# The loop for overfull experts moves from behind step 20 to behind step 4 of the expert stage, and constants move ahead of the first activation

## The chip, the cores and the metric

The kernel runs on one core of one Trainium2 chip. The metric is the device time of one execution in microseconds (us). Three runs of the kernel before took 1916.12, 1918.36 and 1924.67 us; the median is 1918.36 us. In the texts PE is TensorE, DVE is VectorE, ACT is ScalarE, POOL is GpSimd and SP is SyncE; a q behind the name is the engine's sequencer.

## The reference, cut to what matters

Two blocks run one after the other on 256 tokens of 1024 values, all in float32. The first is an attention block with a mixture of experts; the second has two layers, each with a mixer and an MLP. The change lies in the mixture of experts:

```python
logits = t @ w_router + b_router                 # 256 tokens, 32 experts
top_val, top_idx = lax.top_k(logits, 4)          # each token goes to 4 experts
gate_w = softmax(top_val)
# for every expert e and the tokens that chose it:
hb = xb @ w_exp_in[e] + b_exp_in[e]              # 1024 -> 2048
g, u = minimum(hb[:, :1024], 7.0), clip(hb[:, 1024:], -7.0, 7.0)
a = g * sigmoid(1.702 * g) * (u + 1.0)
y = a @ w_exp_out[e] + b_exp_out[e]              # 1024 -> 1024
# every token: the sum of its 4 results by gate_w, then h = layer_norm(alpha * h + sum)
```

The mean load of an expert is 32 tokens, but the router decides, so an expert can have more.

## The kernel before, in words

**The expert stage.** It is written as `step(0)` to `step(32)`. Each step handles one expert with room for 64 tokens (`CAP`); step e also finishes expert e-1. The weights of an expert are six tiles of 2 MiB: four of `w_exp_in` and two of `w_exp_out`. In program order a step uses them as in 0, in 1, out 0 and out 1 of the expert before, in 2, in 3. PE first writes the biases (L771), then multiplies the tokens by the in tiles (`up_tile`, L922, into the banks `pg` and `pu`), turns the activation of the expert before (`aT`, L944), multiplies it by the out tiles (`down_tile`, L953, into `py`), and spreads the result back over all tokens (`combine`, L966, into `pc`), where DVE adds it to the running sum `facc` (L971, written over `bcs`). In every odd step PE also gathers the tokens of the next two experts (`gather`, L895, into `xg`); it needs a selection `sel` that DVE computes (L886). At the end of a step DVE and ACT form the activation (`swiglu`, L932 to L938) and DVE the table `sd` for the way back (L904).

**What sets the order.** PE's instructions of the steps are pinned to program order (`keep`). On DVE, ACT and POOL a scheduler places each instruction, and a tile from a pool can be written only when the readers of the buffer's last user are done. The six weight tiles of a step come through one DMA queue, issued by SP in the order in which `get(key)` asks for them. They rotate through eight buffers of 2 MiB (pools `ring`, `ring2`, `ring3`), so SP can issue a load only when PE has used up the tile that lay in that buffer.

**The loop.** An expert with more than 64 tokens needs further passes. `later_consts` works out from the counts a table `tab` with one entry for each further pass, and their number, which lands in `ti[0:1, 16:17]`. After step 20 the kernel issues the seven loads that follow (all six tiles of step 21, and in 0 of step 22), reads the number into a register of every engine (`values_load`, L1154) and enters a loop with that many trips (`tc.For_i`, L1155). Each trip loads an expert's six tiles through `ring3` and does a whole expert. The loop has an entry and an exit at which the engines meet and the counters of the semaphores start anew. In step 20 the activation and `sd` are kept in another pool (`aside`, pool `accp`), as the loop uses `tmp`.

**What else stands in the stage.** `facc_init` (the start of the running sum; it also takes one step of the side work `ada0`) and `later_consts` (the table, masks and triangles for later stages) are emitted after step 0. `load_bo`, `ln2_rows` and `out_bias` follow steps 2, 4 and 6: the load of `b_exp_out` by POOL, four short rows loaded by POOL and spread over 128 partitions by PE (L1003), and the bias product (L1015).

```python
for e in range(21):                                    # L1144
    step(e)
    if e == 0:
        facc_init()
        later_consts()
    elif e in (2, 4, 6):
        {2: load_bo, 4: ln2_rows, 6: out_bias}[e]()
for key in step_tiles(21) + step_tiles(22)[0:1]:       # L1151
    get(key)
with tc.issue_after(mark["SP"]):
    n_over = nc.values_load(ti[0:1, 16:17], min_val=0, max_val=15)
with tc.For_i(0, n_over, 1) as it:                     # L1155
```

Of the kernel before, what the change touches and what calls it, by code (L numbers as in the profile page):

```python
# [18 lines left out]
NE = 32  # L19
# [53 lines left out]
def tile_kernel(  # L73
# [20 lines left out]
    def bank(name="bank", tag="b"):  # L94
        return pp.tile([128, 512], F32, tag=tag, name=name)
# [31 lines left out]
    def wload(src, shape_str, pool=None, parts=1, pin=False, **kw):  # L127
        s = (pool or ring).tile([128, 4096], F32, tag="w", name="w")
        n = 1
        for d in src.shape[1:]:  # L130
            n *= d
        view = s[:, 0:n].rearrange(shape_str, **kw)
        k = src.shape[1] // parts
        for i in range(parts):
            ins = nc.sync.dma_start(view[:, i * k:(i + 1) * k], src[:, i * k:(i + 1) * k])
            mark["SP"] = ins.ins
            if pin:
                keep(ins)
        return view

    def wcols(w, c0, ncol, k0=0, kc=8, pool=None, parts=1, pin=False):
        return wload(w[k0 * 128:(k0 + kc) * 128, c0:c0 + ncol].rearrange("(k p) n -> p k n", p=128),
                     "p (k n) -> p k n", k=kc, pool=pool, parts=parts, pin=pin)
# [621 lines left out]
    def bias_sel(oh):  # L765
        return oh

    def expert_bias(p, oh, half, pin=lambda i: i, halves=(0, 1)):
        for hv in halves:
            q = 2 * half + hv  # L770
            pin(T.matmul(p[64 * hv:64 * hv + 64, :], oh[:, q:q + 1].to_broadcast([128, 64]), bi,  # L771
                         start=True, stop=False))
# [93 lines left out]
    def step_tiles(e):  # L866

        out = [("in", e, 0), ("in", e, 1)] if e < NE else []
        out += [("out", e - 1, i) for i in range(2)] if e else []
        return out + ([("in", e, 2), ("in", e, 3)] if e < NE else [])  # L870
# [3 lines left out]
    def get(key):  # L874
        if key not in loaded:
            kind, e, i = key
            loaded[key] = spare() if key == ("in", 1, 2) else (tin if kind == "in" else tout)(e, i)
        return loaded[key]

    def gather(rank_aps, pin=lambda i: i):  # L880
        n = len(rank_aps)
        xg = wsp.tile([128, 8, 128], F32, tag="wh", name="xg")
        sel = tmp("sel", 256).rearrange("p (t s) -> p t s", t=2)
        for t in range(2):
            for a in range(n):
                mark["sel"] = V.tensor_scalar(sel[:, t, a * 64:(a + 1) * 64], slot_i, rank_aps[a][:, t:t + 1], None,  # L886
                                              op0=ALU.is_equal).ins
        w = 64 * n

        def half(hf):  # L890
            p = bank("xg")
            for kc in range(4):
                i, r = divmod(4 * hf + kc, 2)
                for t in range(2):
                    pin(T.matmul(p[:, kc * 128:kc * 128 + w], h1[:, t, 256 * i + r:256 * (i + 1):2], sel[:, t, 0:w],  # L895
                                 start=t == 0, stop=t == 1))
            S.copy(xg[:, 4 * hf:4 * hf + 4, 0:w], p.rearrange("p (k s) -> p k s", k=4)[:, :, 0:w])  # L897

        return xg, half
# [17 lines left out]
    def up_tile(acc, xg, a, i, w, pin=lambda i: i):  # L917
        pg_, pu_ = acc
        for r, p, b0 in ((0, pg_, 0), (0, pu_, 1024), (1, pg_, 0), (1, pu_, 1024)) if i < 3 else (
                (0, pg_, 0), (1, pg_, 0), (0, pu_, 1024), (1, pu_, 1024)):  # L920
            for hv in range(2):
                last = pin(T.matmul(p[64 * hv:64 * hv + 64, :], xg[:, 2 * i + r, a * 64:(a + 1) * 64],  # L922
                                    w[:, r, b0 + hv * 512:b0 + (hv + 1) * 512], start=False, stop=i == 3 and r == 1))
        mark["up"] = last.ins
# [16 lines left out]
    def down_turn(uc, pin=lambda i: i):  # L941
        p = bank("aT")
        for r in range(4):
            last = pin(T.transpose(p[:, r * 128:(r + 1) * 128], uc[:, r:512:4], ident))  # L944
        mark["aT"] = last.ins
        aT = tmp("aTs")
        S.copy(aT, p)
        return aT

    def down_tile(py, aT, i, w, pin=lambda i: i):  # L950
        for r in range(4):
            for j in range(2):
                pin(T.matmul(py[64 * j:64 * j + 64, :], aT[:, r * 128 + i * 64:r * 128 + (i + 1) * 64],  # L953
                             w[:, r, j * 512:(j + 1) * 512], start=i == 0 and r == 0, stop=i == 1 and r == 3))

    def evict(py):
        ys = tmp("ys")
        S.copy(ys, py)  # L958
        return ys

    def combine(sT, ys, sums=None, pin=lambda i: i):
        for t in range(2):
            pc = []
            for j in range(2):
                p = sums[t, j] if sums else bank("pc")
                pin(T.matmul(p, sT[64 * j:64 * j + 64, t * 128:(t + 1) * 128], ys[64 * j:64 * j + 64, :],  # L966
                             start=not sums, stop=True))
                pc.append(p)
            for j in range(0 if sums else 2):
                f = facc[:, t, j * 512:(j + 1) * 512]  # L970
                V.tensor_tensor(f, f, pc[j], op=ALU.add)  # L971
# [19 lines left out]
    def facc_init():  # L991
        next(ada0, None)
        with tc.issue_after(first_sel):
            for t in range(2):
                V.tensor_scalar(facc[:, t], h1[:, t], ALPHA, None, op0=ALU.mult)
# [93 lines left out]
    def take_sum(t):  # L1089
        for j in range(2):  # L1090
            p = bank("pc", "bg"[t])
            keep(T.matmul(p, ident, facc[:, t, j * 512:(j + 1) * 512], start=True, stop=False))
            sums[t, j] = p

    def step(e):

        w = {key: get(key) for key in step_tiles(e)}
        d = downs.pop(e - 1, None)
        nxt = None
        if e < NE:  # L1100
            acc = first_acc[e] if e < 2 else (bank("pg", "g"), bank("pu", "g"))
            if e > 1:
                eb = bias_sel(ident[:, 4 * e:4 * e + 4])
                expert_bias(acc[0], eb, 0, keep)
                expert_bias(acc[1], eb, 1, keep)
            xg, a = xgs.pop(e)
            up_tile(acc, xg, a, 0, w["in", e, 0], keep)
            if e == 0:
                with tc.issue_after(mark["up"]):
                    xg_, nxt = gather([rr[:, :, 1]], keep)  # L1110
                xgs[1] = xg_, 0
            elif e % 2 and e + 1 < NE:
                with tc.issue_after(mark["up"]):
                    xg_, nxt = gather([rr[:, :, e + 1 + b] for b in range(2)], keep)
                xgs[e + 1], xgs[e + 2] = (xg_, 0), (xg_, 1)
        if nxt:
            nxt(0)
        if d:
            uc, turn = d
            aT = down_turn(uc, keep)  # L1120
        if e < NE:
            up_tile(acc, xg, a, 1, w["in", e, 1], keep)
        else:
            take_sum(1)
        if d:
            sT = turn()
            py = bank("py")
            for i in range(2):
                down_tile(py, aT, i, w["out", e - 1, i], keep)
            ys = evict(py)  # L1130
        if e < NE:
            up_tile(acc, xg, a, 2, w["in", e, 2], keep)
        if nxt:
            nxt(1)
        if d:
            combine(sT, ys, sums if e == NE else None, keep)
        if e < NE:
            up_tile(acc, xg, a, 3, w["in", e, 3], keep)
            if e == NE - 1:
                take_sum(0)  # L1140
            held = aside if e == 20 else tmp
            downs[e] = swiglu(acc, held), spread_sel(rr[:, :, e], gw[:, :, e], keep, held)

    for e in range(21):  # L1144
        step(e)
        if e == 0:
            facc_init()
            later_consts()
        elif e in (2, 4, 6):
            {2: load_bo, 4: ln2_rows, 6: out_bias}[e]()  # L1150
    for key in step_tiles(21) + step_tiles(22)[0:1]:  # L1151
        get(key)
    with tc.issue_after(mark["SP"]):
        n_over = nc.values_load(ti[0:1, 16:17], min_val=0, max_val=15)  # L1154
    with tc.For_i(0, n_over, 1) as it:  # L1155
# [27 lines left out]
        for i in range(2):  # L1183
            down_tile(py, aT, i, tout(eo, i, ring3, False))
        combine(turn(), evict(py))
    for e in range(21, NE + 1):
        step(e)
    w_ahead = [wcols(w_in_ab_2[0], 2048, 512), wcols(w_in_ab_2[0], 1536, 512), wcols(w_in_ab_2[0], 2560, 512)]
    st2.close()

# [497 lines left out]
```

## Time and profile before

| | |
|---|---|
| three runs | 1916.12, 1918.36, 1924.67 us |
| the profiled execution | 1921.77 us, span 1920.0 us |
| PE busy | 1833.3 us, 95% of the span |
| DVE, ACT, POOL busy | 42%, 29%, 5% |
| data moved by DMA | 595.84 MB, of that 540.68 MB on SP's queue |
| the expert stage | about 253 to 1206 us of the span |

The profile is of one execution; its times count from the start of its span. A group of a timeline gives the start of the first of some like instructions, how long the group took, and in brackets how long the engine had stood idle and what released it. L971 appears once in each step from step 1 on, so the distance from one such row to the next is the length of a step.

### The profile page before, as it was taken

What the parts mean: (1) busy time and instruction counts of PE and PEld (TensorE: products, weight loads), DVE (VectorE), ACT (ScalarE), POOL (GpSimd) and SP (SyncE); (2) the same over time, 40 slices, a digit from 0 to 9 for tenths busy, and PEclk for the clock granted to TensorE, in tenths of its full rate; (3) what the DMA queues carried; (4) which work ended last, traced back from release to release, by engine and by line L of the source; (5) the groups of instructions that cost most, each with busy time, mean ns of one, the idle gap of its engine ahead of it and who ended that gap; (6) DMA issues with size and microseconds to landing.
All of it is one profiled execution on the core that took longest, in us unless ns stands there. A gap on an engine that the chain in (4) does not pass through costs nothing.

```text
span 1920.0 us, 23489 instructions
## 1 busy us (share of the span) xinstructions
PE 1833.3 (95%) x9861; PEld 1106.0 (58%) x9861; DVE 799.4 (42%) x1388; ACT 557.3 (29%) x869; POOL 91.1 (5%) x106
## 2 busy tenths in 40 slices
PE   7999989999999999985999999899999999999999
PEld 6867743333333333322333333688888965778997
DVE  6756741121211221220221122667754465665555
ACT  4645301110011110000101110554544454564443
POOL 3000100000000000000000000200100011000000
PEclk9989979998999999997999999999999999999999
DMA  8667868998999999998999999774666565434452
GB/s 291 243 219 264 346 252 330 428 420 360 425 427 428 427 428 427 428 427 336 427 428 427 428 427 416 268 254 148 250 252 249 213 239 179 153 131 154 176 196 89
DMA packets 100302, 595.84 MB, mean 310 GB/s; under 512 B 7533, under 2 KB 8002, under 8 KB 75362
## 3 DMA queue, kind: packets, MB, share of 16 engines
q1 hardware_dynamic: 85874, 540.68, 69.9%
q0 software_dynamic: 14288, 53.63, 8.0%
q8 instruction: 78, 1.28, 0.3%
q14 instruction: 30, 0.25, 0.0%
q10 hardware_dynamic: 32, 0.01, 0.0%
HBM read 593.24 MB, written 1.06 MB: 310 GB/s over the span
## 4 chain that ended last, share of the span: by engine, by line
PE 80%; DMA 8%; issue 5%; DVE 4%; POOL 1%; ACT 1%; SPq 0%; POOLq 0%; DVEq 0%; ACTq 0%
PE pg L922 11%; PE py L953 11%; PE pu L922 11%; PE xg L895 4%; DMA w<-in_w_exp_in_dram 4%; DMA wa<-in_ada_w_dram 3%; PE hid L271 3%; PE hid L270 3%; PE hid L269 3%; PE pc L966 3%; PE acc L254 3%; PE acc L255 3%; PE acc L256 3%; PE adp L628 2%; PE pu L771 2%
## 5 line engine op out<-in xcount | busy, mean ns | idle before, releaser
L199 DVE TENSOR_TENSOR wl<-w,wh 128x1024 fp32r<-128x1024 f32 x244 | 301.2, 1235 | 231.5 <-ACT wh L198 230.9
L971 DVE TENSOR_TENSOR bcs<-bcs,pc 128x512 f32<-128x512 f32 x124 | 76.9, 682 | 661.5 <-PE pc L966 661.5
L198 ACT CAST wh<-w 128x1024 fp32r<-128x1024 f32 x244 | 255.9, 1049 | 315.3 <-PE acc L256 85.2
L922 PE MATMUL pg<-w,xg 128*64 128x512 f32 x1016 | 262.0, 605 | 1.2 <-DMA w<-in_w_exp_in_dram 1.2
L922 PE MATMUL pu<-w,xg 128*64 128x512 f32 x1016 | 257.1, 595 | 0.0
L953 PE MATMUL py<-w,aTs 128*64 128x512 f32 x1024 | 226.8, 595 | 0.0
L922 PEld LDWEIGHTS pu<-w,xg 128*64 128x64 f32 x1016 | 73.6, 138 | 147.1 <-issue 147.1
L922 PEld LDWEIGHTS pg<-w,xg 128*64 128x64 f32 x1016 | 67.8, 138 | 139.0 <-issue 131.6
L953 PEld LDWEIGHTS py<-w,aTs 128*64 128x64 f32 x1024 | 70.7, 137 | 133.2 <-issue 132.7
L270 PE MATMUL hid<-xhl,wh 128*128 128x256 f32 x512 | 145.4, 284 | 0.0
L271 PE MATMUL hid<-xhl,wl 128*128 128x256 f32 x512 | 145.3, 284 | 0.0
L269 PE MATMUL hid<-xhl,wh 128*128 128x256 f32 x512 | 145.2, 284 | 0.0
L270 PEld LDWEIGHTS hid<-xhl,wh 128*128 128x128 f32 x512 | 98.5, 192 | 2.2 <-issue 1.7
L269 PEld LDWEIGHTS hid<-xhl,wh 128*128 128x128 f32 x512 | 98.5, 192 | 2.1 <-ACT xhl L1255 1.7
L271 PEld LDWEIGHTS hid<-xhl,wl 128*128 128x128 f32 x512 | 98.5, 192 | 0.8 <-issue 0.8
L897 ACT COPY xg<-xg 128x512 f32<-128x512 f32 (+1 forms) x34 | 19.0, 560 | 265.8 <-PE xg L895 265.8
L254 PE MATMUL acc<-wh,hh 128*128 128x512 f32 x240 | 94.5, 394 | 0.0
L255 PE MATMUL acc<-wl,hh 128*128 128x512 f32 x240 | 93.7, 390 | 0.0
L256 PE MATMUL acc<-wh,hh 128*128 128x512 f32 x240 | 93.6, 390 | 0.0
L895 PEld LDWEIGHTS xg<-sel,h 128*128 128x128 f32 x544 | 71.3, 208 | 33.9 <-issue 33.5
L895 PE MATMUL xg<-sel,h 128*128 128x128 f32 (+1 forms) x544 | 77.7, 300 | 6.0 <-DVE sel L886 5.9
L958 ACT COPY ys<-py 128x512 f32<-128x512 f32 x32 | 18.7, 585 | 213.9 <-PE py L953 213.9
(529 smaller groups left out, 2666.7 us busy)
## 6 DMA issues: line engine op xcount, KB each, us to landing
w<-in_w_exp_in_dram SPq DMA_DIRECT2D x125, 2048.0 KB, 16.5
w<-in_w_exp_out_dram SPq DMA_DIRECT2D x63, 2048.0 KB, 13.4
w<-in_mlp_w_dram SPq DMA_DIRECT2D x32, 2048.0 KB, 7.5
wa<-in_ada_w_dram POOLq DMA_DIRECT2D x38, 1024.0 KB, 7.4
w<-in_w_in_dram SPq DMA_DIRECT2D x9, 2048.0 KB, 10.0
w<-in_w_in_ab_dram SPq DMA_DIRECT2D x7, 2048.0 KB, 13.8
w<-in_w_qkv_dram SPq DMA_DIRECT2D x6, 2048.0 KB, 7.8
wa<-in_ada_w_dram POOLq DMA_DIRECT2D x20, 512.0 KB, 4.8
```

Source lines behind the costliest of these rows:

```text
L198: mark["S"] = S.copy(hi, src).ins
L199: mark["V"] = V.tensor_tensor(lo, src, hi.bitcast(F32), op=ALU.subtract).ins
L254: T.matmul(outs[t], hs, wh[:, j, :], start=a, stop=False)
L255: T.matmul(outs[t], hs, wl[:, j, :], start=False, stop=False)
L256: T.matmul(outs[t], ls, wh[:, j, :], start=False, stop=z)
L269: T.matmul(o, hs, xh[:, k + j, :], start=a, stop=False, skip_group_check=True)
L270: T.matmul(o, hs, xl[:, k + j, :], start=False, stop=False, skip_group_check=True)
L271: last = T.matmul(o, ls, xh[:, k + j, :], start=False, stop=z and m % 2 == 1, skip_group_check=True)
L895: pin(T.matmul(p[:, kc * 128:kc * 128 + w], h1[:, t, 256 * i + r:256 * (i + 1):2], sel[:, t, 0:w], start=t == 0, stop=t == 1))
L922: last = pin(T.matmul(p[64 * hv:64 * hv + 64, :], xg[:, 2 * i + r, a * 64:(a + 1) * 64], w[:, r, b0 + hv * 512:b0 + (hv + 1) * 512], start ...
L953: pin(T.matmul(py[64 * j:64 * j + 64, :], aT[:, r * 128 + i * 64:r * 128 + (i + 1) * 64], w[:, r, j * 512:(j + 1) * 512], start=i == 0 and ...
L971: V.tensor_tensor(f, f, pc[j], op=ALU.add)
```

## The change

The loop now stands behind step 4 (`LOOP_STEP`), with the seven loads ahead of it now those of step 5 and of in 0 of step 6, and with step 4's activation in `accp`. `facc_init` and `later_consts` are emitted inside step 0, ahead of its `swiglu`. `load_bo`, `ln2_rows` and `out_bias` follow steps 6, 8 and 10.

```diff
             up_tile(acc, xg, a, 3, w["in", e, 3], keep)
             if e == NE - 1:
                 take_sum(0)
-            held = aside if e == 20 else tmp
+            if e == 0:
+                facc_init()
+                later_consts()
+            held = aside if e == LOOP_STEP else tmp
             downs[e] = swiglu(acc, held), spread_sel(rr[:, :, e], gw[:, :, e], keep, held)
 
-    for e in range(21):
+    LOOP_STEP = 4
+    for e in range(LOOP_STEP + 1):
         step(e)
-        if e == 0:
-            facc_init()
-            later_consts()
-        elif e in (2, 4, 6):
-            {2: load_bo, 4: ln2_rows, 6: out_bias}[e]()
-    for key in step_tiles(21) + step_tiles(22)[0:1]:
+    for key in step_tiles(LOOP_STEP + 1) + step_tiles(LOOP_STEP + 2)[0:1]:
         get(key)
 ...
-    for e in range(21, NE + 1):
+    for e in range(LOOP_STEP + 1, NE + 1):
         step(e)
+        if e in (6, 8, 10):
+            {6: load_bo, 8: ln2_rows, 10: out_bias}[e]()
```

On SP the loop's entry stood behind the loads of step 21 and now stands behind those of step 5 (`ti` holds the number of trips; lines below 1154 are one lower after the change). This is the new place, + is the kernel after:

```order
 L135 DMA w<-in_w_exp_in_dram 128x4096 x4
 L135 DMA w<-in_w_exp_out_dram 128x4096 x2
+L135 DMA w<-in_w_exp_in_dram 128x4096 x3
+L1153 TENSOR_LOAD ti
+L1154 COMPARE_AND_BRANCH
+L1154 UNCONDITIONAL_BRANCH x2
+L1685 BRANCH_PREFETCH_HINT
+L1155 ISA
```

The same rows, from the entry to the end of the loop's body, are gone from their old place; the order of the weight loads among themselves is the same.

On DVE, at the end of step 0, this stood before; `gc`, `uc` and `sg` are the activation, `ia`, `ib` and `masks` the constants, `sel` the selection for the gather in step 1:

```order
301 L1085 TENSOR_SCALAR lbl<-lbl 128x4
302 L932 TENSOR_SCALAR gc<-pg 128x512
303 L937 TENSOR_SCALAR uc<-pu 128x512
304 L904 TENSOR_SCALAR sd<-slot_i,rr,gw 128x128 x2
305 L935 TENSOR_TENSOR sg<-sg,gc 128x512
...
309 L1042 TENSOR_TENSOR ia<-slot_i,pre 128x512
310 L1043 TENSOR_TENSOR ib<-slot_i,cum 128x512
...
340 L1071 TENSOR_TENSOR masks<-masks,u_lt 128x128
341 L886 TENSOR_SCALAR sel<-slot_i,rr 128x64
```

And this stands there now:

```order
284 L1065 TENSOR_SCALAR ri<-row_i 128x1
285 L1042 TENSOR_TENSOR ia<-slot_i,pre 128x512
286 L1043 TENSOR_TENSOR ib<-slot_i,cum 128x512
...
326 L1071 TENSOR_TENSOR masks<-masks,u_lt 128x128
...
331 L1085 TENSOR_SCALAR lbl<-lbl 128x4
332 L932 TENSOR_SCALAR gc<-pg 128x512
333 L937 TENSOR_SCALAR uc<-pu 128x512
...
339 L938 SCALAR_TENSOR_TENSOR uc<-uc,sg 128x512
340 L886 TENSOR_SCALAR sel<-slot_i,rr 128x64 x4
```

The constants stood between the activation of expert 0 and the selection for the next gather, the last masks among the four selections; now they stand ahead of the activation, and the selection follows it at once.

On POOL, where `bo` is the load of `b_exp_out` and `jp`, `col` are index tables from which the masks are made, the rows at the start of the stage change like this:

```order
-L834 DMA bo<-in_b_exp_out_dram 32x512
 L189 TENSOR_TENSOR ln1r<-rsq_v,mhalf 128x1 x2
 L811 TENSOR_TENSOR h_82<-x_tm,bcs 128x1024
 L813 TENSOR_TENSOR h_82<-h_82,bcs 128x1024 x2
 L1061 IOTA row_i 128x1
-L834 DMA bo<-in_b_exp_out_dram 32x512
-L1055 IOTA jp_2365 128x128
+L1055 IOTA jp_2354 128x128
 L1059 IOTA col 128x128
```

The load that stood ahead of the two index tables is now behind the loop.

## Rows read from the trace of the kernel before

**Rows 1.** Timeline of DVE, L971 of steps 2, 3, 4, 7, 19, 20 and 21.

```profile
332.10 2.48 DVE L971 TENSOR_TENSOR bcs<-bcs,pc 128x512 f32<-128x512 f32 x4 [19.20 <-PE pc L966]
361.79 2.48 DVE L971 TENSOR_TENSOR bcs<-bcs,pc 128x512 f32<-128x512 f32 x4 [22.42 <-PE pc L966]
387.52 2.48 DVE L971 TENSOR_TENSOR bcs<-bcs,pc 128x512 f32<-128x512 f32 x4 [19.20 <-PE pc L966]
...
491.62 2.48 DVE L971 TENSOR_TENSOR bcs<-bcs,pc 128x512 f32<-128x512 f32 x4 [27.50 <-PE pc L966]
...
824.14 2.48 DVE L971 TENSOR_TENSOR bcs<-bcs,pc 128x512 f32<-128x512 f32 x4 [22.44 <-PE pc L966]
851.25 2.48 DVE L971 TENSOR_TENSOR bcs<-bcs,pc 128x512 f32<-128x512 f32 x4 [20.57 <-PE pc L966]
914.87 2.48 DVE L971 TENSOR_TENSOR bcs<-bcs,pc 128x512 f32<-128x512 f32 x4 [27.66 <-PE pc L966]
```

**Rows 2.** Timeline of PE from step 20 into step 21.

```profile
846.50 1.08 PE L922 MATMUL pg<-w,xg 128*64 128x512 f32 x4 [1.16 <-DMA w<-in_w_exp_in_dram]
...
853.77 1.89 PE L922 MATMUL pu<-w,xg 128*64 128x512 f32 x8
886.57 1.98 PE L771 MATMUL pg<-bi,ident 128*64 128x512 f32 x4 [30.91 <-issue]
...
890.04 1.92 PE L922 MATMUL pg<-w,xg 128*64 128x512 f32 x4
```

**Rows 3.** Chain of waits, 840 to 892 us: start us, us, what.

```profile
850.20 35.36 DMA w<-in_w_exp_in_dram
885.56 1.01 issue
```

**Rows 4.** DMA, 531 to 831 us, SP's queue: packets, MB, share of 16 engines.

```profile
q1 hardware_dynamic: 8791, 128.06, 100.4%
```

**Rows 5.** Windows: us; PE, PEld, DVE, ACT, POOL busy; PEclk, DMA share, GB/s.

```profile
460.00:480.00 20.00, 20.00 (x76) 7.52 (x77) 2.06 (x3) 1.48 (x3) 0.00 (x0) 0.78 0.70 266
...
831.00:851.00 20.00, 18.84 (x88) 6.25 (x86) 0.00 (x0) 1.54 (x3) 0.00 (x0) 1.00 1.01 428
```

**Rows 6.** DMA, 471 to 850.6 us: SP's queue, and its issues.

```profile
q1 hardware_dynamic: 11008, 160.45, 99.8%
...
w<-in_w_exp_in_dram SPq DMA_DIRECT2D x55, 2048.0 KB, 22.4
w<-in_w_exp_out_dram SPq DMA_DIRECT2D x28, 2048.0 KB, 21.2
```

**Rows 7.** The same, 289 to 386.9 us.

```profile
q1 hardware_dynamic: 2568, 37.57, 92.9%
...
w<-in_w_exp_in_dram SPq DMA_DIRECT2D x15, 2048.0 KB, 13.7
w<-in_w_exp_out_dram SPq DMA_DIRECT2D x6, 2048.0 KB
```

**Rows 8.** Timelines of SP and PE: step 4's load of in 0 for step 6, its last product.

```profile
386.47 0.33 SPq L135 DMA_DIRECT2D w<-in_w_exp_in_dram  x1
...
390.05 1.89 PE L922 MATMUL pu<-w,xg 128*64 128x512 f32 x8
```

**Rows 9.** Timeline of DVE, 246 to 285 us.

```profile
254.98 0.17 DVE L1085 TENSOR_SCALAR lbl<-lbl 128x4 f32<-128x4 f32 x1
272.07 0.69 DVE L932 TENSOR_SCALAR gc<-pg 128x512 f32<-128x512 f32 x1 [16.92 <-PE pg L922]
...
276.31 0.69 DVE L1042 TENSOR_TENSOR ia<-slot_i,pre 128x512 f32<-128x512 f32 x1
...
284.77 0.25 DVE L886 TENSOR_SCALAR sel<-slot_i,rr 128x64 f32<-128x64 f32 x1
```

**Rows 10.** Timeline of PE, the two gather halves of step 1.

```profile
284.23 4.09 PE L895 MATMUL xg<-sel,h 128*128 128x128 f32 x16 [5.93 <-DVE sel L886]
...
303.13 2.15 PE L895 MATMUL xg<-sel,h 128*128 128x128 f32 x16
```

**Rows 11.** Timeline of POOL: the second load of `bo`, then the index tables.

```profile
275.02 0.58 POOL L834 DMA_DIRECT2D bo<-in_b_exp_out_dram  x1 [32.56 <-PE ada L587]
275.61 0.25 POOL L1055 IOTA jp<- 128x128 int32 x1
```

## Prediction, made before the change was run

> **What bounds the kernel now.** I first looked for the length of a step. L971 runs once in a step, and its starts lie 25.73 us apart into an even step and 29.69 us into an odd one, which has the gather (361.79 to 387.52, and 332.10 to 361.79) [rows 1]. A pair of steps is 55.42 us, a step 27.71 us on average. This holds up to step 19; PE waits for nothing there and is the bound. The reader is to see three places where it does not hold. Into step 20 it is 27.11 us, 1.38 us too long: PE waits for a weight tile, 1.16 us of it in one place [rows 1, 2]. Into step 21 it is 63.62 us (851.25 to 914.87), 33.93 us too long, of which 30.91 us are an idle PE between the last product of step 20 and the bias product of step 21 [rows 1, 2]. Nothing stands in between: the loop has no trip, and all of this is its entry and exit. The third is in step 1, where PE idles 5.93 us for the selection from DVE, told with the constants below.
>
> Next, what the loop waits for. The chain of waits goes through one load, issued at 850.20 and landed 35.36 us later, and 1.01 us after that PE starts [rows 3]. So the engines leave only when the last prefetched tile has landed. Why does a 2 MiB load take 35 us? DMA is the slower partner. From 531 to 831 us the queue moved 128.06 MB in 300 us, 426.9 GB/s [rows 4]; a step's six tiles are 12.58 MB, which take 29.48 us, 1.77 us more than PE needs. The eight buffers hide that for a time: each step the loads fall 1.77 us further behind. After `out_bias`, which stopped the loads for lack of a free buffer (266 GB/s in its window, 428 later) [rows 5], the buffers were full; 14 steps later, in step 20, PE waits for the first time. The loop stands just where the loads are furthest behind.
>
> **The change part by part.** The sum is made against the profiled execution, 1921.77 us (span 1920.0), which is 3.4 us over the median of the runs, 1918.36.
>
> *The loop.* It must wait for the same seven loads, but at step 4 fewer bytes are still under way. From 471 us, when nothing was under way, to 850.6 us, 83 loads (55 and 28) were issued, 174.06 MB, and 160.45 were moved: 13.61 MB left, 31.9 us at 426.9 GB/s, so 882.5; the chain says 885.56, 3.1 us later [rows 3, 4, 6]. From 289 us, when again nothing was under way, to 386.9, just behind the load that would be the last one ahead of the new loop (in 0 of step 6, at 386.47), 21 loads were issued, 44.04 MB, and 37.57 moved: 6.47 MB left, 15.2 us [rows 7, 8]. With the same 3.1 us the last tile lands at 405.2, and with 1.01 us PE starts at 406.2. PE ends step 4 at 390.05 + 1.89 = 391.94 [rows 8]. It would idle 14.2 us in place of 30.91: **16.7 us gained**. Bounds: with no 3.1 us the stop is 11.1 (19.8 gained); if something else holds the loop as long as now, nothing is gained. I take 16.7, worked out like the stop that is known. Both stops leave PE at half clock for a while (four products of L922 in 1.92 us at 890.04, 1.08 at 846.50) [rows 2], so that cancels. The part of DVE and ACT in step 4 ends while the loads are still landing; `aside` costs nothing.
>
> *The constants.* At step 1 DVE finished the activation, then did the constants from 276.31 to 284.77 + 0.25, with the four selections among the last of them, and PE waited 5.93 us; its gather then took 4.09 us for 16 products, against 2.15 in the other half [rows 9, 10]. Now the constants stand ahead of the activation, where DVE idles 16.92 us until 272.07 [rows 9]. The 8.7 us of constants fit. The index tables that they need were held up on POOL behind the load of `bo` until 275.61 [rows 11]; that load is now behind the loop. The selection follows the activation at about 277, and the gather is wanted at 278.3 (284.23 less 5.93). **Gained 5.93 + 1.94 = 7.9 us.** Bounds: 7.9; and nothing, if the constants wait until some 270 us for a `tmp` buffer that the gather of step 0 reads, since then the selection is where it was. More than that could be lost only if they came after 272. I take 7.9, as the idle time is twice the work.
>
> *The moved loads and products.* `ln2_rows` and `out_bias` cost PE what they cost before, four steps later; `load_bo` is two short loads that nobody waits for before step 10. Nothing, unless the rows' loads wait longer on POOL; their place on the queue is the same.
>
> *What is late next: the end of the stage.* Here a part is given back. The loop emptied the queue at step 20, which filled all the buffers, and the 11 steps behind it never waited. In the kernel after, the buffers are filled at the loop, and again by `out_bias` behind step 10. From there the pattern of before runs again four steps later: 14 steps, and in step 24 PE waits, with the 1.38 us that step 20 has now. Steps 25 to 31 then go at the pace of the loads: 7 steps at 1.77 us, **12.4 us lost**. The last expert's work follows its last tile and is not hidden. Bounds: nothing, if the loads keep up; 20 us if each wait also brings the half clock (below).
>
> Sum: -16.7 - 7.9 + 12.4 = -12.2 us: 1909.6 against the profiled execution, **1906.2 us** against the median. The stages behind the experts keep their order and time.
>
> **A rule that speaks against it.** PE waiting for tiles in steps 25 to 31 is new. The row: in the window 831 to 851 us, with the 1.16 us wait, the granted clock was 1.00 (2.4 GHz) [rows 2, 5], while the 30.91 us stop brought it down. The Trainium skill (TensorE: Matmul & The Clock Gate, section "HAM oscillation — how this bites in real kernels") says that waits for DMA between tiles throttle PE so that each tile starts at the low clock. By the row the tail costs 12.4 us; what the rule would make of it is the third rival.
>
> **The rivals.**
> 1. The constants do not get out of the way: they end late enough that PE still waits. Speaks for it: they share eight `tmp` buffers with the selections. Against: 16.92 us of idle DVE ahead of 272.07 [rows 9]. Half of the gain left gives -8.3 us, 1910; none of it -4.3, 1914.
> 2. The end of the stage is not bound by the loads, or by less. For: PE's 1.77 us a step is a small difference of two large numbers. Against: PE did run dry 14 steps after full buffers, and 21 steps follow here. With half the loss: -18.4, 1900; with none -24.6, 1894.
> 3. The low clock in the tail. Products at half clock take some 1.7 us for four in place of 0.86, and the stretch behind the loop cost 33.93 - 30.91 = 3.0 us [rows 1, 2]. If every step of the seven paid 3.0, a step of PE would be 30.7 us, 1.2 over the loads: 8.6 more, -3.6 in all, 1915. Against: a PE behind the loads finds full buffers and no more waits, which ends it.
> 4. The other side: the loop's stop does not depend on how far the loads are behind, but costs 31 us wherever it stands (its seven loads could be issued later relative to PE than I read, or the meeting itself be slow). Then -7.9 + 12.4 = 4.5 us slower, 1923. It decides from a stop of 26.4 us on (30.91 - 4.5); against it, the chain puts all but 1.01 us on the load [rows 3].
>
> **How the numbers follow.** A change of 0.5% (9.6 us) is about what a measurement of this kernel can tell from none. My forecast: 0.58, with its own range 1902 to 1911 (gains of 7 to 16 us), some four fifths of it past 9.6 us. Rival 1: 0.14, nearly all within 0.5%. Rival 2: 0.13, all faster. Rival 3: 0.08, within. Rival 4: 0.07, half of it within, half slower. Faster: 0.46 + 0.13 + 0.02 = 0.61; slower 0.04, with 0.01 for what I have not seen, 0.05; the same 0.34. The range leaves out the far ends of rivals 2 and 4: 1896 to 1917.
>
> **What would show it.** Right: one stop of PE of 13 to 15 us between steps 4 and 5, at about 384 to 398 us, with a load as its releaser; no idle PE ahead of the gather of step 1, and L971 of step 4 near 380; lengths of 25.73 and 29.69 us up to step 23, then about 29.5 for steps 25 to 31, with PE waiting for `w_exp_in` and `w_exp_out` for 10 to 15 us in sum; PEclk 1.00 there. Wrong: a stop over 25 us; a selection still late at step 1; the last steps at 27.7 us on average (then rival 2), or at half clock (rival 3).

## The result and the profile after

The kernel after took 1909.51 us, the median of 8 runs (1899.68 to 1914.16); the kernel before had a median of 1922.44 us over its 8 runs, 12.9 us more, where 12.2 us were forecast. One of these eight took 3699.66 us; without it the median is 1920.21, 10.7 us over the kernel after, and the ratio is 0.9935, 95% interval [0.9914, 0.9955]: 0.65% faster. The profiled executions are 8.55 us apart (1913.22 and 1921.77 us; spans 1911.4 and 1920.0).

The lengths of the steps come first, as in [rows 1]: the timeline of DVE in the kernel after, L971 of steps 1, 4, 5, 23, 24, 25, 30 and 31.

```profile
300.26 2.48 DVE L971 TENSOR_TENSOR bcs<-bcs,pc 128x512 f32<-128x512 f32 x4 [21.07 <-PE pc L966]
...
381.42 2.48 DVE L971 TENSOR_TENSOR bcs<-bcs,pc 128x512 f32<-128x512 f32 x4 [19.19 <-PE pc L966]
426.78 2.48 DVE L971 TENSOR_TENSOR bcs<-bcs,pc 128x512 f32<-128x512 f32 x4 [26.77 <-PE pc L966]
...
943.46 2.48 DVE L971 TENSOR_TENSOR bcs<-bcs,pc 128x512 f32<-128x512 f32 x4 [22.44 <-PE pc L966]
969.62 2.48 DVE L971 TENSOR_TENSOR bcs<-bcs,pc 128x512 f32<-128x512 f32 x4 [19.62 <-PE pc L966]
1001.91 2.48 DVE L971 TENSOR_TENSOR bcs<-bcs,pc 128x512 f32<-128x512 f32 x4 [25.04 <-PE pc L966]
...
1146.99 2.48 DVE L971 TENSOR_TENSOR bcs<-bcs,pc 128x512 f32<-128x512 f32 x4 [20.73 <-PE pc L966]
1175.04 2.48 DVE L971 TENSOR_TENSOR bcs<-bcs,pc 128x512 f32<-128x512 f32 x4 [21.45 <-PE pc L966]
```

Step 5 takes 45.36 us, 15.67 over its 29.69: that is the loop, 33.93 before. Up to step 23 only the steps with `ln2_rows` and `out_bias` (9 and 11) are longer than 25.73 or 29.69 besides. In step 24 the tail begins: 26.16 in place of 25.73, then 32.29 (step 25), and 28.05 in the last. The eight steps 24 to 31 are 13.85 us too long in sum (step 31 has no gather and counts as 25.73).

Now the stop, against [rows 2, 3], and the gather of step 1, against [rows 10]. Timeline of PE, kernel after:

```profile
280.07 2.15 PE L895 MATMUL xg<-sel,h 128*128 128x128 f32 x16
...
383.94 1.89 PE L922 MATMUL pu<-w,xg 128*64 128x512 f32 x8
399.38 1.98 PE L771 MATMUL pg<-bi,ident 128*64 128x512 f32 x4 [13.55 <-issue]
401.14 1.92 PE L771 MATMUL pu<-bi,ident 128*64 128x512 f32 x4
402.85 1.23 PE L922 MATMUL pg<-w,xg 128*64 128x512 f32 x4
403.91 1.02 PE L922 MATMUL pu<-w,xg 128*64 128x512 f32 x4
```

Chain of waits, kernel after, at the stop:

```profile
380.37 18.00 DMA w<-in_w_exp_in_dram
398.36 1.02 issue
```

PE idles 13.55 us; again it is one load, here landed after 18.00 us, and 1.02 us behind it PE starts. The half clock behind the stop is over at 403.91, some 4.5 us after its end. Ahead of the gather of step 1 nothing idles any more, and the 16 products take 2.15 us. The reason is on DVE (kernel after; compare [rows 9]):

```profile
258.74 0.29 DVE L1071 TENSOR_TENSOR masks<-masks,u_lt 128x128 int32<-128x128 int32 x1
...
277.86 0.68 DVE L938 SCALAR_TENSOR_TENSOR uc<-uc,sg 128x512 f32<-128x512 f32 x1
278.46 0.74 DVE L886 TENSOR_SCALAR sel<-slot_i,rr 128x64 f32<-128x64 f32 x4
```

The last mask is done at 259.0, in time that DVE used to spend idle, and the selections follow the activation. PE's waits for weight tiles in the whole run (line, releaser: us in total, times, longest), kernel after:

```profile
PE pg L922 <- DMA w<-in_w_exp_in_dram: 7.7, 7, 1.2
...
PE py L953 <- DMA w<-in_w_exp_out_dram: 3.3, 4, 1.1
```

These eleven waits, 11.0 us, are the tail. The window 1000 to 1140 us (columns as in [rows 5]), kernel after, lies in it:

```profile
1000.00:1140.00 140.00, 134.53 (x643) 49.97 (x644) 29.20 (x58) 13.09 (x24) 0.00 (x0) 1.00 1.01 428
```

PE is busy 96% there, the granted clock is 1.00, and DMA runs at 428 GB/s, the rate of the stretches in which it never stops.

### The profile page after: what moved, and what is told of

Same layout as the page of the kernel before. It is cut to its first block, busy times and chain, and to the rows that moved or that the text cites. A ratio compares the mean times of both kernels' runs of the same rounds, so it can differ in the third digit from the quotient of the medians.

```text
span 1911.4 us, 23485 instructions
## 1 busy us (share of the span) xinstructions
PE 1837.3 (96%) x9861; PEld 1103.7 (58%) x9861; DVE 798.8 (42%) x1388; ACT 557.6 (29%) x869; POOL 91.7 (5%) x106
## 4 chain that ended last, share of the span: by engine, by line
PE 71%; DMA 10%; DVE 3%; issue 2%; ACT 1%; POOL 1%; POOLq 0%; DVEq 0%; ACTq 0%
PE pg L922 11%; PE pu L922 10%; PE py L953 10%; DMA w<-in_w_exp_in_dram 6%; PE xg L895 4%; PE hid L271 3%; PE hid L270 3%; PE hid L269 3%; PE acc L254 3%; PE acc L255 3%; PE acc L256 3%; PE pc L966 3%; DMA wa<-in_ada_w_dram 2%; DMA w<-in_w_exp_out_dram 2%; PE adp L628 1%
## 5 line engine op out<-in xcount | busy, mean ns | idle before, releaser
L971 DVE TENSOR_TENSOR bcs<-bcs,pc 128x512 f32<-128x512 f32 x124 | 76.9, 682 | 672.9 <-PE pc L966 672.9
L922 PE MATMUL pg<-w,xg 128*64 128x512 f32 x1016 | 262.5, 606 | 7.7 <-DMA w<-in_w_exp_in_dram 7.7
L922 PE MATMUL pu<-w,xg 128*64 128x512 f32 x1016 | 256.5, 594 | 0.0
L922 PEld LDWEIGHTS pu<-w,xg 128*64 128x64 f32 x1016 | 73.3, 138 | 147.3 <-issue 147.3
L922 PEld LDWEIGHTS pg<-w,xg 128*64 128x64 f32 x1016 | 67.2, 138 | 147.6 <-issue 125.4
## 6 DMA issues: line engine op xcount, KB each, us to landing
w<-in_w_exp_in_dram SPq DMA_DIRECT2D x125, 2048.0 KB, 17.5
```

## The experiments

Two theories. **S**, the prediction's: the time is a sum of terms of PE (stop, constants, tail). **L**: from the loop on the loads set the time; the stage takes its bytes at 428 GB/s plus the time in which the DMA engines stand idle, and a shorter wait of PE is worth only the DMA idle time that goes with it. L got this form after runs 1 to 4. Medians below are to be held against 1909.51 us (after) and 1920 to 1922 us (before); the ratios are to the kernel before, measured beside each.

**1. The loop alone, and 2. the constants alone.**

```diff
# e1: kernel after, constants where they were
-            if e == 0:
-                facc_init()
-                later_consts()
     for e in range(LOOP_STEP + 1):
         step(e)
+        if e == 0:
+            facc_init()
+            later_consts()
# e2: kernel before, only these three lines moved into step 0
```

> The loop and the later loads stand where the change puts them, the constants where they stood before. Theory (the terms add up): the selection for step 1 is late again, PE idles about 6 us ahead of the gather of step 1, the stop between steps 4 and 5 stays at 13 to 14 us and the tail waits at 13 to 14 us in sum; 7.9 us over the changed kernel, so about 5 us under the kernel before. Rival (the loads decide the whole stage, and PE time won early is given back at its end): the time of the changed kernel, within 2 us, with a stop or a tail shorter by some 6 us.

> Only the constants move; the loop stays behind step 20 and the rows' loads behind steps 2 to 6. Theory: no idle PE ahead of the gather of step 1, the stop behind step 20 as long as before (30 to 31 us), no waits in the last steps; 7.9 us under the kernel before. Rival (the loads decide): the 7.9 us reappear as a longer stop or as waits ahead of step 20, and the time is that of the kernel before, within 2 us.

The loop alone: 1916.42 us, ratio 0.9983 [0.9965, 1.0000], hardly to be told from no change; the constants alone: 1912.66 us, 0.9968 [0.9950, 0.9986]. So in medians the constants are worth 6.9 us (1916.42 less 1909.51) and 9.0 us (1921.63 less 1912.66; by the interval 2.7 to 9.6), the forecast 7.9 between the two. Timeline of PE, loop alone:

```profile
286.10 4.19 PE L895 MATMUL xg<-sel,h 128*128 128x128 f32 x16 [5.93 <-DVE sel L886]
...
408.67 1.98 PE L771 MATMUL pg<-bi,ident 128*64 128x512 f32 x4 [13.72 <-issue]
```

The 5.93 us are back to the digit, and the stop is the same. Timeline of PE, constants alone:

```profile
272.83 2.15 PE L895 MATMUL xg<-sel,h 128*128 128x128 f32 x16
...
873.86 1.98 PE L771 MATMUL pg<-bi,ident 128*64 128x512 f32 x4 [31.71 <-issue]
```

No wait at the gather, and the old stop. Time won at step 1 is not given back, so the rival of these two runs is out. L does not speak against that, as the DMA engines had stood still for the late selection too: from 290 to 330 us they move 300 GB/s with the loop alone and 374 in the kernel after, 6.9 us of idle time at 428, while at the loop and at `out_bias` the two kernels show the same 366 and 398.

**3. Without the loop, and 4. the rows late.**

```diff
# e3: kernel after, values_load and For_i with its body left out
# e4: kernel after
-        if e in (6, 8, 10):
-            {6: load_bo, 8: ln2_rows, 10: out_bias}[e]()
+        if e in (6, 18, 24):
+            {6: load_bo, 18: ln2_rows, 24: out_bias}[e]()
```

> The changed kernel without the loop: the passes for overfull experts are left out (these inputs have none). Theory: the stop and the half clock behind it go (15.7 us in the profile of the changed kernel), the buffers are still filled at the bias product behind step 10, and the tail waits stay at 13 to 14 us: 15 to 16 us under the changed kernel. Rival: the stop was time in which the loads caught up; without it PE runs dry earlier, and 10 us or more come back as waits in the last steps: 0 to 6 us under the changed kernel.

> The changed kernel with ln2_rows behind step 18 and out_bias behind step 24 in place of 8 and 10. Theory (the tail is short of loads because the loads fall 1.77 us a step behind from the last point at which the buffers were full): the buffers are full at the loop, PE would run dry 14 steps later, at step 19; the 8 and 10 us of PE work put in there give the loads time, so that PE waits for tiles only 3 to 6 us in sum in place of 13.9; 8 to 11 us under the changed kernel. Rival (the tail waits are of the end of the stage, its last tiles or its place, and do not depend on when the buffers were full): waits of 12 to 15 us remain, and the time is that of the changed kernel within 2 us.

Without the loop: 1891.99 us, 0.9859 [0.9832, 0.9885], 17.5 us under the kernel after: the theory's number, a little more. With the rows late: 1904.83 us, 0.9925 [0.9897, 0.9953]. The direction is the theory's, but 4.7 us are half of what it expected, and the intervals of the two versions overlap; in the profiles the time from L971 of step 1 to that of step 31 is 5.96 us shorter. PE ran dry in step 18 (26.76 in place of 25.73 us), in steps 22 to 24 and again in 30 and 31, 9.7 us too long in sum. So the place of the tail depends on when the buffers were last full, but the gain was wrongly sized.

Which of S and L? Windows of DMA tell. Kernel after, at the loop and at `out_bias`:

```profile
370.00:430.00 60.00, 46.45 (x218) 17.77 (x216) 9.28 (x19) 4.12 (x8) 1.09 (x2) 0.89 0.91 366
...
520.00:620.00 100.00, 97.78 (x448) 37.52 (x444) 20.46 (x39) 8.71 (x16) 0.00 (x0) 0.95 0.96 398
```

Without the loop:

```profile
370.00:430.00 60.00, 60.00 (x292) 22.89 (x290) 11.80 (x24) 5.55 (x11) 1.09 (x2) 1.00 1.01 424
...
520.00:620.00 100.00, 97.78 (x446) 36.59 (x442) 21.07 (x41) 8.80 (x16) 0.00 (x0) 0.97 1.01 428
```

With the rows late:

```profile
370.00:430.00 60.00, 46.40 (x220) 17.81 (x218) 10.44 (x21) 4.46 (x8) 1.09 (x2) 0.89 0.92 368
...
520.00:620.00 100.00, 100.00 (x482) 37.56 (x480) 20.21 (x39) 9.18 (x17) 0.00 (x0) 1.00 1.01 428
```

Against 428 GB/s, the kernel after leaves (428 - 366) / 428 of 60 us unused at the loop, 8.7 us, and 7.0 us at `out_bias`. Without the loop 0.6 and nothing; with the rows late 8.4 and nothing. Without the loop the idle time at `out_bias` is gone as well: the loads are then further behind there. The next runs were chosen where S and L differ.

**5 to 8. Fewer loads ahead of the loop.** `step_tiles(LOOP_STEP + 1) + step_tiles(LOOP_STEP + 2)[0:1]` are seven loads.

```diff
# e5: kernel after; e6: the same with [0:5], on the version with the rows late
-    for key in step_tiles(LOOP_STEP + 1) + step_tiles(LOOP_STEP + 2)[0:1]:
+    for key in (step_tiles(LOOP_STEP + 1) + step_tiles(LOOP_STEP + 2))[0:4]:
# e7: both edits of e3 and e4
# e8: kernel before, loop behind step 20
-    for key in step_tiles(21) + step_tiles(22)[0:1]:
+    for key in step_tiles(21)[0:1]:
```

> The changed kernel with four loads ahead of the loop in place of seven. Both theories: the fourth load has landed before PE ends step 4 (at 383.7 us against 385.8 in the profile of the changed kernel), so the stop shrinks from 13.55 us to 1 to 3 us (if a loop's entry and exit cost that much by themselves; if the stop were the price of a loop, it would stay at 13 us). Theory S (a sum of PE's terms): the 11 us are won, the tail waits stay at 13.9 us: 1897 to 1899 us. Theory L (from step 2 on the stage takes its bytes at 428 GB/s plus the time in which the DMA engines idle): at the loop they idle some 6 us in place of 8.6, and behind the bias product of step 10 some 0 to 1 in place of 6.9, since the loads are further behind there; 8 to 9 us won, 1900 to 1902 us, with 16 to 18 us of tail waits.

> Five loads ahead of the loop, ln2_rows behind step 18 and out_bias behind step 24. The fifth load lands at 388.6 us in the profile of the changed kernel, so the stop is about 4 us. Theory S: against the version with the late rows and seven loads (1904.8 us) the stop's 10 us are won: 1895 us. Theory L: at the loop the DMA engines idle 3 to 4 us in place of 8.6, nothing else changes: 5 us won, 1900 us, and PE waits some 5 us more for tiles than with seven loads (7.7 us there).

> The changed kernel without the loop (the passes for overfull experts are left out; these inputs have none) and with ln2_rows behind step 18, out_bias behind step 24. Theory S: the late rows win here what they won with the loop, 5 to 6 us: 1886 us. Theory L: without the loop the DMA engines already never idle from 310 us to the end of the stage, so there is nothing to win: 1892 us within 2 us, with the tail waits of that version (13.0 us) spread over other steps.

> The kernel before, with one load (in 0 of step 21) ahead of the loop in place of seven; the loop stays behind step 20. Theory L: the stop shrinks from 30.9 us to 1 to 3 us, as the first of the seven lands about when PE ends step 20; the steps behind the loop go at the pace of the loads (29.5 us) from step 22 on, so PE waits some 15 to 18 us for tiles; 12 to 14 us under the kernel before. Rival (a loop costs some 30 us at this place whatever is under way): the stop stays over 25 us, and the time is that of the kernel before or more.

Four ahead: 1901.66 us, 0.9904 [0.9887, 0.9922]. Five ahead with the rows late: 1901.06 us, 0.9894 [0.9875, 0.9913]. No loop and the rows late: 1892.23 us, 0.9840 [0.9818, 0.9862]. In medians all three are at L's numbers (1900 to 1902, 1900, 1892), not at S's (1897 to 1899, 1895, 1886), though two of the five executions of the last (1886.15 and 1886.37) are at S's. The old place with one load ahead: 1911.81 us, 0.9951 [0.9933, 0.9969], 10.3 us under its kernel before, where 12 to 14 were expected.

The stops of PE (timelines): four ahead,

```profile
388.77 1.08 PE L771 MATMUL pg<-bi,ident 128*64 128x512 f32 x4 [2.69 <-DVEq L1154]
```

five ahead with the rows late,

```profile
390.37 1.98 PE L771 MATMUL pg<-bi,ident 128*64 128x512 f32 x4 [4.88 <-issue]
```

and the old place with one ahead:

```profile
855.10 1.89 PE L922 MATMUL pu<-w,xg 128*64 128x512 f32 x8
863.25 1.97 PE L771 MATMUL pg<-bi,ident 128*64 128x512 f32 x4 [6.26 <-DMA w<-in_w_exp_in_dram]
```

So the stop is the landing of the last load issued ahead, behind step 4 as behind step 20. With four ahead all had landed: DMA moves nothing from 383 to 385 us. The 2.69 us that are left have a sequencer at the loop's own line as releaser, DVE's, and DVE comes to the loop from step 4's activation and `sd` (last row of them, timeline of DVE, four ahead):

```profile
387.92 0.34 DVE L904 TENSOR_SCALAR sd<-slot_i,rr,gw 128x128 f32<-128x128 f32 x1
```

It is done 0.51 us before PE goes on, so by the profile most of the 2.69 us is a wait for DVE and not a price of the loop. At step 20 even the first of the loads was late, hence 6.26 us and not the 1 to 3 expected; and as PE waits there for the loads anyway, the stop of 30.91 us shrank by 24.7 us and the time by 10.3.

DMA at the same two windows, four ahead:

```profile
370.00:430.00 60.00, 57.30 (x270) 21.59 (x268) 11.90 (x24) 5.42 (x10) 1.09 (x2) 0.97 0.87 356
...
520.00:620.00 100.00, 97.78 (x448) 36.51 (x446) 20.46 (x39) 8.60 (x16) 0.00 (x0) 0.97 1.01 428
```

Five ahead with the rows late:

```profile
370.00:430.00 60.00, 55.12 (x258) 20.84 (x256) 11.90 (x24) 5.05 (x9) 1.09 (x2) 0.94 0.92 378
```

No loop and the rows late:

```profile
370.00:430.00 60.00, 60.00 (x292) 22.82 (x290) 11.81 (x24) 5.42 (x10) 1.09 (x2) 1.00 1.01 424
```

The table holds the time from L971 of step 1 to L971 of step 31 (as 300.26 to 1175.04 above) against the DMA idle time of these windows (a rate of 427 or 428 counts as full):

| kernel | PE's stop, us | steps 1 to 31, us | DMA idle: loop + `out_bias`, us | difference |
|---|---|---|---|---|
| after | 13.55 | 874.78 | 8.7 + 7.0 | 859.1 |
| no loop | none | 860.24 | 0.6 + 0 | 859.7 |
| rows late | 13.6 | 868.82 | 8.4 + 0 | 860.4 |
| four ahead | 2.69 | 869.87 | 10.1 + 0 | 859.8 |
| five ahead, rows late | 4.88 | 867.35 | 7.0 + 0 | 860.3 |
| no loop, rows late | none | 861.44 | 0.6 + 0 | 860.9 |

The stop ranges from nothing to 13.6 us and the stage by 14.5 us, but less the idle time it is 859.1 to 860.9 in every row. Four ahead cut step 5 by 11.06 us (45.36 to 34.30) and the stage by 4.91; the DMA engines stood still longer at the loop (10.1 us against 8.7) and not at all at `out_bias`. That is L, and S would have won 11. Each row is one execution.

Two things limit this. The last column is close to bookkeeping: 364.7 to 365.3 MB move on SP's queue between the two rows of L971 in every version of the table, so a time less the DMA idle time has to come out alike; it shows only that idle time differs nowhere else (the 4.7 to 5.0 us at 290 to 330 us are in every row). And L's forecasts of the idle time at the loop were wrong: some 6 us with four ahead, where 10.1 came, and 3 to 4 with five ahead and the rows late, where 7.0 came. So the stage got shorter by 4.91 and 1.47 us, less than the 8 to 9 and 5 that L foresaw, and the medians (7.9 and 3.8) fit L better than the profiles do. What stands is that S is out: it would have won 11 and 10. The trace shows what L's forecasts left out: with few loads ahead DMA runs out of work, and SP, which stands at the loop too, issues the next load only on leaving it. With four ahead DMA moves at most 37 GB/s in any 2 us from 382 to 390 us, and that load is issued at 388.99.

**9 and 10. The loop behind step 0.** At 250 to 260 us of the kernel after DMA is still in any case (at most 2 GB/s).

```diff
# e9: rows late; e10: rows late and [0:5] as in e6
-    LOOP_STEP = 4
+    LOOP_STEP = 0
```

> The loop behind step 0, seven loads ahead of it, ln2_rows behind step 18 and out_bias behind step 24. At 250 to 260 us of the changed kernel the DMA engines stand still with full buffers, so the loop comes when next to nothing is under way: the last of its seven loads is issued when PE ends step 0 (275.6 us) and lands some 9 us later, a stop of 9 to 10 us. Theory L: the DMA engines idle some 8 us at this stop, but the 5 us that they stood still at 290 to 330 us go (the stop fills the buffers at nearly the same place): against the late rows with the loop behind step 4 (1904.8 us), where the idle time was 13 us, some 3 to 5 us won: 1900 to 1902 us. Theory S (the sum of PE's terms): the stop is 4 us shorter, 1901 us, and no tail waits less.

> The same with five loads ahead of the loop. The fifth is issued when PE has used up the third tile of step 0 (about 266 to 270 us) and lands at 275 to 280 us: a stop of 3 to 5 us. Theory L: the DMA engines idle some 6 to 7 us at the loop in place of 8: 1898 to 1901 us. Theory S: 5 to 6 us less than with seven loads: 1895 us.

They took 1899.34 and 1899.45 us, both 0.9892 [0.9875, 0.9909], the lowest medians with the loop in place: 10 us under the kernel after, though not measured side by side with it. The stop was wrongly foreseen: most of the seven tiles already lay in the buffers (SP issued two loads between 250 and 280 us), and the longest idle time of PE around the loop is this one (timeline, seven ahead):

```profile
282.38 2.77 PE L895 MATMUL xg<-sel,h 128*128 128x128 f32 x16 [2.15 <-DVE sel L886]
```

That selection had itself waited 2.1 us for the loop (L1154). The medians do not decide between the theories here: 1899.34 lies just under L's 1900 to 1902 and under S's 1901. The windows of DMA, seven ahead:

```profile
260.00:290.00 30.00, 27.85 (x146) 13.81 (x142) 4.91 (x17) 3.94 (x7) 0.59 (x1) 0.94 0.65 246
290.00:330.00 40.00, 40.00 (x192) 15.03 (x192) 5.72 (x11) 3.72 (x7) 0.50 (x1) 1.00 1.01 421
```

The version with the rows late and the loop behind step 4 moves 397 and 378 GB/s there. So the drain does not fall into the stretch in which DMA is still anyway but just behind it: it costs 10.6 us of idle time from 260 to 290 us, and saves 4.0 us from 290 to 330 and the 8.4 us around the old loop. That is 1.8 us in sum, and the profile has L971 of step 31 2.3 us earlier (1165.24 against 1167.52); the medians are 5.5 us apart. Five loads ahead in place of seven change nothing, as hardly any load is under way: PE's wait is 2.15 us there too. S's 1895 was built on a stop that did not come, so this run does not test S.

## Why the prediction was right, step by step

**The time and the sum.** 1906.2 was forecast, 1909.5 measured, inside the range. In medians -12.2 stands against -12.9. That these are so close is in part luck: against the median of the three runs from which the forecast was made, 1918.36 us, the kernel after is 8.9 us faster, by the profiles 8.6, while the terms below, as measured, come to 14.8.

**The loop.** A stop of 14.2 us was worked out from bytes issued and moved, 13.55 measured, and its releaser is the load. That it costs the same anywhere (rival 4) is refuted by the stops of 2.69 to 31.71 us above. The half clock behind the stop did not cancel: 3.0 us before, 2.1 after (15.67 - 13.55). The term is 33.93 - 15.67 = 18.3 in place of 16.7: the mechanism as forecast, the size 1.6 us short.

**The constants.** 7.9 forecast. By the profiles the lag of the kernel after goes from +1.83 us at L922 of step 1 (276.48 against 274.65) to -6.10 behind the gather (282.06 against 288.16): 7.9. The bound "nothing", constants held by a `tmp` buffer until 270 us, did not come: they are done at 259. Rival 1 is out.

**The moved rows.** Costed at nothing; the two steps were 7.55 + 11.44 us longer before and 8.15 + 9.74 after, 1.1 us gained. With the constants alone, which leaves these rows at their old place, the two steps were 9.85 + 9.74 longer, so this is no effect of the place that could be told from scatter; behind `out_bias` it is a shorter half clock (four products of L922 in 1.92 us before, 1.39 after).

**The tail.** Forecast: dry in step 24, then the pace of the loads, 12.4 us lost, 10 to 15 us of waits. Measured: dry in step 24, 13.85 us, of which the 1.38 us of step 20 are only moved: 12.5 lost, 29.35 us a step from step 25 on, and 11.0 us of waits. Rival 2 is out. Rival 3 too: in the window 1000 to 1140 us the clock is 1.00 with PE idle 5.5 us in it. The Trainium skill (TensorE: Matmul & The Clock Gate, "HAM oscillation — how this bites in real kernels") tells of a kernel in which each tile starts at the low clock behind a wait for DMA of about 3 to 5 us. The waits in this trace are at most 1.2 us, so it shows no such drop and does not contradict that page either; the prediction took the page's rule further than its case.

**The rest of the profile.** -18.3 - 7.9 - 1.1 + 12.5 = -14.8 us, and the stage indeed ends 12.98 us earlier having been 1.83 late. The spans differ by 8.6 only: from L971 of step 31 to the end the kernel after needed 736.4 us and the kernel before 732.0. Over the twelve profiles that stretch took 728.6 to 736.4 us, with the same 4330 products of PE in it. Windows of it, kernel after, then kernel before:

```profile
1175.04:1911.40 736.36, 712.04 (x4330) 581.46 (x4326) 440.60 (x620) 353.07 (x489) 55.13 (x65) 0.98 0.56 201
1188.02:1920.00 731.98, 708.01 (x4330) 579.95 (x4326) 441.00 (x620) 352.93 (x489) 54.46 (x65) 0.99 0.56 200
```

Of the 4.4 us 4.0 are PE's busy time, at a lower granted clock; in the shortest (four ahead, 728.62 us) PE is busy 703.80 us and the clock is 1.00. Why it differs from one execution to the next stays open.

**What the prediction did not see.** It added the terms as if each stood alone. That was right in sum because it had priced the tail, where the loads give the time back. For the loop this is most of the gain: 18.3 us less 12.5. L says why: the DMA engines stand still about as long around the new place (8.7 us) as around the old one (362 GB/s from 840 to 900 us, 9.3 us). For the constants nothing comes back, as DMA idle time went with the wait. And terms do not go on adding up: as soon as the idle time at `out_bias` is used up, as with four loads ahead, the next gain of PE comes back as a wait in the tail. By L the price of the loop that is left is not PE's 13.55 us but the 8.7 us of DMA idle time around it, and those of `out_bias` behind it; without the loop both are gone and the stage is 14.5 us shorter.

## What to carry to other kernels

Where two partners are as close as here (27.71 us of PE, 29.5 us of loads a step), count the idle time of both: PE's wait is only worth what DMA's idle time shrinks with it, once the buffers run dry before the end. A stop that drains a queue costs the time in which the queue stands still around it, so ask what other idle time it takes the place of; the best place tried was the one behind step 0, by 2.3 us in the profiles. Short work that blocks the buffers' release makes the loads wait where the buffers are full: put late, where the loads were behind, it was worth 5.96 us of the stage here with the loop (4.7 in medians, within their noise) and nothing without it. Before moving a stop, ask how many bytes are under way at it: here its length was their landing.

## What the runs showed of the hardware beyond that

At an empty loop with nothing under way PE stopped 2.69 us here, most of it for DVE's part of the step; what the loop costs by itself no run shows. Draining the queue behind step 4 left DMA idle for 7.0 to 10.1 us, more than the stop of PE where few loads were ahead (10.1 against 2.69, 7.0 against 4.88), as SP issues nothing until it leaves the loop.

The same instructions at the same place can meet either clock. The first gather, x32, in the kernel after (granted clock 0.50 from 250 to 254 us, 1.2 GHz):

```profile
247.68 7.09 PE L895 MATMUL xg<-sel,h 128*128 128x64 f32 x32
```

and with the constants alone (1.00 there, 2.4 GHz):

```profile
246.13 3.95 PE L895 MATMUL xg<-sel,h 128*128 128x64 f32 x32
```

Eleven of the twelve profiles show the half clock there, one the full clock, and L971 of step 1 starts 5.6 us or more earlier in that one than in all the others (293.02 against 298.62 to 309.38 us). No effect of the change was seen in it. It may be a part of the 14 us over which the runs of the kernel after scatter; only profiles show the clock, so that is not shown.
